# B11 + B12 in a seven-product SwiGLU matmul: the vector engine's addition replaced by a DMA transfer that adds on arrival

## The chip, the cores and the metric

The kernel runs on one core of one Trainium2 chip. The metric is the device time of one execution in microseconds. A core has a matrix engine (PE), a vector engine (DVE), a scalar engine (ACT), GpSimd (POOL) and SyncE (SP). Each works through its own list of instructions in order and waits at the head of that list for semaphores of the others. Transfers are issued from the lists of SP, ACT or POOL and are carried out by 16 DMA engines that all of them share.

## The reference, cut to what matters

One layer of a trunk with 512 latent tokens and 256 context tokens of width 2048. The change lies in the channel mixer, in the first product of `swiglu`, whose weight is 2048 x 11264 (5632 columns for `a`, 5632 for `b`):

```python
def swiglu(h, w_in, w_out):
    a, b = jnp.split(h @ w_in, 2, axis=-1)
    return (jax.nn.silu(a) * b) @ w_out

def trunk_layer(...):
    ...
    x = x + mod_x[2] * rms_norm(y_x, g_post_mix)
    f_x = swiglu(modulate(rms_norm(x, g_pre_ffn), mod_x[3], mod_x[4]), w_ffn_in, w_ffn_out)
    x = x + mod_x[5] * rms_norm(f_x, g_post_ffn)
```

## The kernel before

The layer runs stage by stage: modulation vectors, input projections, the gated linear attention, the output projection (`wo`, to about 930 us of the span), the first SwiGLU product (`f0` to `f10`, about 950 to 1850 us), the second one (`fo`, `fz`, to the end). Every float32 operand is split into a rounded high part and a remainder (`parts`, L992 to L997: ACT casts the high part, DVE subtracts for the low part), and each product is three matmuls: high by high, low by high, high by low.

The first SwiGLU product is cut into 11 groups of 512 columns of `a` and the 512 columns of `b` beside them (`ffn_group(gi)`, tiles named `f0...` to `f10...`). In a group the weight is a 2 x 2 matrix of blocks: B11 and B21 are the upper and lower 1024 rows of the `a` columns, B12 and B22 those of the `b` columns. The tokens are cut in two halves as well. The 2 x 2 product is made with seven block products in place of eight, from sums of blocks; the sums of the activations (`S1` to `S7`) are made once, those of the weights in every group. Each block comes in four pieces q = 0 to 3 of 256 rows, and a piece is one SBUF tile of 128 x 1024 float32, 512 KB, loaded by one transfer issued from SP (`wide`, L999, through `load`, L195).

The products of a group and the names of their pieces, in order:

- product 1, from B11: `X` is loaded and its parts are `a0` to `a3`. Groups 0 to 2 have products 1 (and mostly 2) done early, from another copy of the block; there `X` is only loaded, ahead of the sum.
- product 2, from B21: `b0` to `b3`.
- product 5, from B11 + B12: `c` is loaded and added into `X` (L1225); the parts of `X` are now `c0` to `c3`.
- product 6: `d` (B22) is added into `X` (L1232). Product 4: `e` (B21 again) is added into `X` (L1241).
- products 3 and 7: `z` (B22) and `y` (B12), with one sum `y + z` (L1255).

Four sets of buffers set the pace: `X` has 4 tiles, the loaded pieces `R` (for b, c, d, e, z, y) have 4, and the high and the low parts have 3 each. A load waits until its buffer's last reader is done, and so does a cast into a part's buffer, whose last reader is PE. A background generator (`gate_ffn`) reads more weight rows (`m50w` to `m53w`) between the groups; its accumulators are cleared by a memset on POOL.

The order in which each engine does its work is written when the program is built, by a scheduler that goes by the program's order, by the buffers that are free and by modelled durations.

Of the kernel before, what the change touches and what calls it, by code (L numbers as in the profile page):

```python
# [15 lines left out]
ALU = mybir.AluOpType  # L16
AX = mybir.AxisListType

P = 128
# [6 lines left out]
HID = 5632  # L26
# [65 lines left out]
def trunk_kernel(ctx, tc, cmat, cmask, x, c, ctxt, c_ctx, w_mod, b_mod, g_pre_mix, g_post_mix, g_pre_ffn,  # L92
                 g_post_ffn, w_in, ln_g, ln_b, w_s, b_s, wd2_f, bd_f, wd2_b, bd_b, out_g, w_out, w_ffn_in,
                 w_ffn_out, out):
    nc = tc.nc
    V, S, T, G = nc.vector, nc.scalar, nc.tensor, nc.gpsimd
# [64 lines left out]
    def rstd_exp(ss, n, name):  # L161

        s1 = cp.tile([P, n], F32, tag=f"s{n}", bufs=4, name=name + "s")
        v = cp.tile([P, n], F32, tag=f"rv{n}", bufs=2, name=name + "v")
        r = cp.tile([P, n], F32, tag=f"rr{n}", bufs=4 if n == 1 else 2, name=name + "r")
        t = cp.tile([P, n], F32, tag=f"rt{n}", bufs=2, name=name + "t")
        V.tensor_reduce(out=s1, in_=ss, axis=AX.X, op=ALU.add)
        S.activation(r, s1, AF.Ln, bias=eps, scale=1.0 / D)
        S.activation(r, r, AF.Exp, scale=-0.5)
        V.tensor_scalar(out=v, in0=s1, scalar1=1.0 / D, scalar2=EPS, op0=ALU.mult, op1=ALU.add)  # L170
        newton(v, r, t)
        return r
# [108 lines left out]
    def pump():  # L281
        bg.step()
        bgm.step()
# [406 lines left out]
    for o in (0, 512):  # L690
        n = min(512, len(LEVELS) * P - o)
# [290 lines left out]
    def fslot(name, dt=F32):  # L982
        return fp.tile([P, 512], dt, tag="f", bufs=NF, name=name)

    def chain_tile(name):
        return fp.tile([P, 1024], F32, tag="X", bufs=4, name=name)

    def raw2(name):
        return st2.tile([P, 1024], F32, tag="R", bufs=4, name=name)

    def parts(src, name):

        wh = st2.tile([P, 1024], F32R, tag="wh", bufs=3, name=name + "h")
        wl = st2.tile([P, 1024], F32R, tag="wl", bufs=3, name=name + "l")
        S.copy(wh, src)  # L995
        V.tensor_tensor(out=wl, in0=src, in1=wh.bitcast(F32), op=ALU.subtract)  # L996
        return wh, wl  # L997

    def wide(w, r, c0, t, name):  # L999

        load(t.rearrange("p (k c) -> p k c", k=2), w[r:r + 2 * P, c0:c0 + 512].rearrange("(k p) c -> p k c", p=P))
        return t
# [145 lines left out]
    def product(p, q, accs, wp, nq):  # L1148
        hi, lo = SP[p][q]
        for j in range(2):  # L1150
            for t in range(2):
                c = slice(j * 256 + t * P, j * 256 + (t + 1) * P)
                three(accs[t], (hi[:, c], lo[:, c]), cut(wp, j * 512, 512), q == 0 and j == 0, q == nq - 1 and j == 1)

    def two(name):
        return [bank(f"{name}{t}") for t in range(2)]
# [5 lines left out]
    def vtt(out, a, b, op):  # L1162
        for i in range(2):
            V.tensor_tensor(out=out[i], in0=a[i], in1=b[i], op=op)

    def blk(gi, i, j, q, t):

        return wide(w_ffn_in[0], i * (D // 2) + 2 * q * P, (gi * 512, HID + gi * 512)[j], t, f"f{gi}")

    def ffn_top(gi, new):  # L1170

        n = f"f{gi}"
        raw = [None] * NQ
        ps = two(n + "p1")
        for q in range(NQ):
            raw[q] = blk(gi, 0, 0, q, new(f"{n}X{q}"))
            product(1, q, ps, parts(raw[q], f"{n}a{q}"), NQ)
            pump()
        u = [fslot(f"{n}u{t}") for t in range(2)]
        for t in range(2):  # L1180
            S.copy(u[t], ps[t])
        turn_hidden()
        return u, raw

    def ffn_top2(gi, u):

        n = f"f{gi}"
        ps = two(n + "p2")
        for q in range(NQ):
            product(2, q, ps, parts(blk(gi, 1, 0, q, raw2(f"{n}b{q}")), f"{n}b{q}"), NQ)  # L1190
            pump()
        a1 = [fslot(f"{n}g{t}") for t in range(2)]
        vtt(a1, ps, u, ALU.add)
        for t in range(2):
            S.activation(a1[t], a1[t], AF.Silu)
        turn_hidden()
        return a1
# [15 lines left out]
    def ffn_group(gi):  # L1213
        n = f"f{gi}"
        if gi >= 3:
            u, X = ffn_top(gi, chain_tile)
        else:
            u = early_u[gi]
            X = [blk(gi, 0, 0, q, chain_tile(f"{n}X{q}")) for q in range(NQ)]
        a1 = ffn_top2(gi, u) if gi >= 2 else early_a[gi]  # L1220

        p5 = two(n + "p5")
        for q in range(NQ):
            r = blk(gi, 0, 1, q, raw2(f"{n}c{q}"))
            V.tensor_tensor(out=X[q], in0=X[q], in1=r, op=ALU.add)  # L1225
            product(5, q, p5, parts(X[q], f"{n}c{q}"), NQ)
            pump()
        turn_hidden()
        p6 = two(n + "p6")
        for q in range(NQ):  # L1230
            r = blk(gi, 1, 1, q, raw2(f"{n}d{q}"))
            V.tensor_tensor(out=X[q], in0=X[q], in1=r, op=ALU.add)  # L1232
            product(6, q, p6, parts(X[q], f"{n}d{q}"), NQ)
            pump()
        vtt(u, u, p6, ALU.subtract)
        u4 = [fslot(f"{n}w{t}") for t in range(2)]
        vtt(u4, p5, u, ALU.add)
        p4 = two(n + "p4")
        for q in range(NQ):
            r = blk(gi, 1, 0, q, raw2(f"{n}e{q}"))  # L1240
            V.tensor_tensor(out=X[q], in0=X[q], in1=r, op=ALU.add)  # L1241
            product(4, q, p4, parts(X[q], f"{n}e{q}"), NQ)
            pump()
        vtt(u, p4, u, ALU.add)
        if gi == HID // 512 - 1:
            for _ in range(8):
                gT.append(next(src))

        p7, p3 = two(n + "p7"), two(n + "p3")
        for q in range(NQ):  # L1250
            z = blk(gi, 1, 1, q, raw2(f"{n}z{q}"))
            y = blk(gi, 0, 1, q, raw2(f"{n}y{q}"))
            product(3, q, p3, parts(z, f"{n}z{q}"), NQ)
            pump()
            V.tensor_tensor(out=y, in0=y, in1=z, op=ALU.add)  # L1255
            product(7, q, p7, parts(y, f"{n}y{q}"), NQ)
        vtt(u, u, p7, ALU.subtract)
        for t in range(2):
            S.activation(u[t], u[t], AF.Silu)
        vtt(p7, p7, u4, ALU.subtract)  # L1260
        vtt(u4, p3, u4, ALU.subtract)
        vtt(a1, a1, u4, ALU.mult)
        vtt(u, u, p7, ALU.mult)
        behind.append((gi, a1 + u))
# [3 lines left out]
    def turn_hidden():  # L1268

        while behind:  # L1270
            gi, toks = behind.pop()
            n = f"f{gi}"
            for f in range(4):
                ps = bank(f"{n}T{f}", False)
                for t in range(NT):
                    T.transpose(ps[:, t * P:(t + 1) * P], toks[t][:, f * P:(f + 1) * P], ident)
                gt = slot(f"{n}t{f}")
                S.copy(gt, ps)
                nc.scalar.dma_start(g_dr[gi * 4 + f], gt)
# [8 lines left out]
    for gi in range(HID // 512):  # L1288
        if gi == 3:
            bgm.add(gate_ffn())  # L1290
        ffn_group(gi)
# [51 lines left out]
    for t in range(NT):  # L1343
# [5 lines left out]
        for cg in range(4):  # L1349
# [3 lines left out]
            f = facc[t][cg]  # L1353
# [4 lines left out]
        r = rstd_exp(fss, 1, f"er{t}")  # L1358
# [32 lines left out]
```

## Time and profile before

| | |
|---|---|
| median of 3 runs | 2351.94 us (2342.42 to 2353.6) |
| the profiled execution's own time | 2349.05 us |
| its span | 2347.2 us |
| PE busy | 2262.3 us (96%) |
| PE weight loads busy | 1836.9 us (78%) |
| DVE busy | 1593.5 us (68%) |
| ACT busy | 982.2 us (42%) |
| POOL busy | 15.5 us (1%), 24 instructions |
| moved by DMA | 477.30 MB, mean 203 GB/s |

The busy time of an engine is given for the whole span. Stages have different limits, so the rows below are taken stretch by stretch. PE's matmuls overlap, and a PE row's busy time counts their modelled ends; PE's real losses show as waits and in the granted clock.

### The profile page before, as it was taken

How to read it: one execution, taken by the hardware profiler on the slowest of the kernel's cores; microseconds unless marked ns; L12 is line 12 of the kernel's file. 1: busy time of each engine (PE TensorE's matmuls, PEld its weight loads, DVE VectorE, ACT ScalarE, POOL GpSimd, SP SyncE). 2: the span in 40 equal slices, each digit the busy share in tenths (PEclk: the TensorE clock that was granted, in tenths of full speed). 3: DMA queues.
4: the chain of work that ended last, by engine and by line, in shares of the span. 5: the costliest groups of instructions: out<-in, count | busy, mean ns of one | idle time of the engine just before them, and what ended most of it. 6: DMA issues, size and time to landing. Idle time of an engine off the chain costs nothing.

```text
span 2347.2 us, 27855 instructions
## 1 busy us (share of the span) xinstructions
PE 2262.3 (96%) x10386; PEld 1836.9 (78%) x10386; DVE 1593.5 (68%) x2072; ACT 982.2 (42%) x1509; POOL 15.5 (1%) x24
## 2 busy tenths in 40 slices
PE   7999998999999989989999999999999999999998
PEld 2778887788878867767788877788888788888886
DVE  3886587677795655798878877887888732242346
ACT  4444234465565315853444444344444432241232
POOL 0000000000000000000000000000000000000000
PEclk9999999999999999999999999999999999999999
DMA  9967788844452785756666756776686642253344
GB/s 324 329 217 236 239 294 275 266 159 126 155 182 86 251 286 182 226 186 225 218 210 220 244 192 209 248 232 203 199 261 198 234 144 98 93 182 104 109 139 156
DMA packets 252012, 477.30 MB, mean 203 GB/s; under 512 B 21162, under 2 KB 32642, under 8 KB 251876
## 3 DMA queue, kind: packets, MB, share of 16 engines
q1 hardware_dynamic: 241152, 457.78, 59.6%
q10 hardware_dynamic: 10724, 17.74, 2.1%
q8 instruction: 81, 1.33, 0.2%
q14 instruction: 55, 0.45, 0.1%
HBM read 451.33 MB, written 24.13 MB: 203 GB/s over the span
## 4 chain that ended last, share of the span: by engine, by line
PE 64%; DMA 15%; DVE 15%; issue 3%; ACT 2%; SPq 0%; DVEq 0%; ACTq 0%
PE fo L116 19%; PE wo L116 4%; PE f1p L116 3%; PE f9p L116 3%; PE f2p L116 3%; PE vv1a L116 2%; PE u1a L116 2%; PE fz L116 2%; PE cv L116 2%; PE g1a L116 2%; PE f7p L116 2%; PE q L116 2%; PE vv0a L116 2%; PE u L116 2%; PE g0a L116 2%
## 5 line engine op out<-in xcount | busy, mean ns | idle before, releaser
L1207 DVE TENSOR_TENSOR gl<-gr,gh 128x512 fp32r<-128x512 f32 x44 | 28.4, 686 | 24.7 <-ACT gh L1206 24.7
L1206 ACT CAST gh<-gr 128x512 fp32r<-128x512 f32 x44 | 25.1, 618 | 33.3 <-DMA gr<-g_dr 26.4
L832 ACT ACTIVATE lv<-lv 128x1024 f32<-128x1024 f32 x20 | 21.0, 1057 | 21.6 <-DVE lv L831 21.6
L229 DVE SCALAR_TENSOR_TENSOR m20acc<-m20w,cpair,m20acc 128x1024 f32<-128x1024 f32 x16 | 20.5, 1284 | 12.6 <-DMA m20w<-in_w_mod_dram 12.4
L996 DVE TENSOR_TENSOR fo_2l<-fo_r,fo_2h 128x1024 fp32r<-128x1024 f32 x8 | 9.8, 1225 | 27.0 <-ACT fo_2h L995 27.0
L116 PE MATMUL g1a<-hxh,g_0h 128*128 128x512 f32 x64 | 27.4, 429 | 0.3 <-ACT g_0h L277 0.3
L996 DVE TENSOR_TENSOR fo_8l<-fo_r,fo_8h 128x1024 fp32r<-128x1024 f32 x8 | 9.8, 1226 | 26.2 <-ACT fo_8h L995 26.2
L116 PE MATMUL vv0a<-vv_0h,hxh 128*128 128x512 f32 x64 | 27.6, 434 | 0.0
L996 DVE TENSOR_TENSOR fo_18l<-fo_r,fo_18h 128x1024 fp32r<-128x1024 f32 x8 | 9.8, 1226 | 26.1 <-ACT fo_18h L995 26.1
L996 DVE TENSOR_TENSOR fo_0l<-fo_r,fo_0h 128x1024 fp32r<-128x1024 f32 x8 | 9.8, 1223 | 25.5 <-ACT fo_0h L995 25.5
L1355 ACT ACTIVATE junk<-fc 128x512 bf16<-128x512 f32 x16 | 10.1, 631 | 40.4 <-DVE fc L1354 40.3
L116 PEld LDWEIGHTS s<-lv 128*128 128x128 f32 x192 | 25.0, 191 | 2.4 <-issue 0.5
L116 PE MATMUL g0a<-hxh,g_0h 128*128 128x512 f32 x64 | 26.8, 419 | 0.0
L996 DVE TENSOR_TENSOR fo_16l<-fo_r,fo_16h 128x1024 fp32r<-128x1024 f32 x8 | 9.8, 1225 | 24.7 <-ACT fo_16h L995 24.7
L116 PE MATMUL vv1a<-vv_0h,hxh 128*128 128x512 f32 x64 | 26.3, 426 | 0.0
L996 DVE TENSOR_TENSOR fo_10l<-fo_r,fo_10h 128x1024 fp32r<-128x1024 f32 x8 | 9.8, 1224 | 24.1 <-ACT fo_10h L995 24.1
L116 PE MATMUL vv0a<-vv_0l,hxh 128*128 128x512 f32 x64 | 26.1, 408 | 0.0
L116 PE MATMUL vv0a<-vv_0h,hxl 128*128 128x512 f32 x64 | 26.0, 407 | 0.0
L996 DVE TENSOR_TENSOR fo_14l<-fo_r,fo_14h 128x1024 fp32r<-128x1024 f32 x8 | 9.8, 1224 | 23.9 <-ACT fo_14h L995 23.9
L229 DVE SCALAR_TENSOR_TENSOR m21acc<-m21w,cpair,m21acc 128x1024 f32<-128x1024 f32 x16 | 20.5, 1282 | 7.9 <-DMA m21w<-in_w_mod_dram 7.3
L996 DVE TENSOR_TENSOR fo_12l<-fo_r,fo_12h 128x1024 fp32r<-128x1024 f32 x8 | 9.8, 1226 | 23.5 <-ACT fo_12h L995 23.5
L116 PE MATMUL g0a<-hxh,g_0l 128*128 128x512 f32 x64 | 25.7, 402 | 0.0
(3875 smaller groups left out, 7969.8 us busy)
## 6 DMA issues: line engine op xcount, KB each, us to landing
fo_r<-in_w_ffn_out_dram SPq DMA_DIRECT2D x80, 512.0 KB
gr<-g_dr SPq DMA_DIRECT2D x22, 512.0 KB
mx4w<-in_w_mod_dram SPq DMA_DIRECT2D x16, 512.0 KB
mx8w<-in_w_mod_dram SPq DMA_DIRECT2D x16, 512.0 KB
mx12w<-in_w_mod_dram SPq DMA_DIRECT2D x16, 512.0 KB
mc4w<-in_w_mod_dram SPq DMA_DIRECT2D x16, 512.0 KB
mc8w<-in_w_mod_dram SPq DMA_DIRECT2D x16, 512.0 KB
mc12w<-in_w_mod_dram SPq DMA_DIRECT2D x16, 512.0 KB
```

The lines of the kernel that those rows point to most:

```text
L116: return T.matmul(o, lhsT=l, rhs=r, start=start, stop=stop)
L229: ins = V.scalar_tensor_tensor(out=acc, in0=raw[:, j].rearrange("p i c -> p (i c)"), scalar=cvec[:, k0 + j:k0 + j + 1], in1=acc, op0=ALU.m ...
L832: S.activation(lv, lv, AF.Exp)
L996: V.tensor_tensor(out=wl, in0=src, in1=wh.bitcast(F32), op=ALU.subtract)
L1206: S.copy(hi, r[:, j * 512:(j + 1) * 512])
L1207: V.tensor_tensor(out=lo, in0=r[:, j * 512:(j + 1) * 512], in1=hi.bitcast(F32), op=ALU.subtract)
L1355: S.activation(junk, f, AF.Square, accum_out=fss[:, cg:cg + 1])
```

## The change

In each of the 11 groups the four loads of `c` from SP into an `R` buffer and the four additions on DVE go. In their place POOL issues four transfers that read the same 512 KB of B12 and add it to what stands in `X`. What followed, the parts `c0` to `c3` and product 5, is as it was.

```diff
         p5 = two(n + "p5")
         for q in range(NQ):
-            r = blk(gi, 0, 1, q, raw2(f"{n}c{q}"))
-            V.tensor_tensor(out=X[q], in0=X[q], in1=r, op=ALU.add)
+            nc.gpsimd.dma_start(X[q].rearrange("p (k c) -> p k c", k=2),
+                                w_ffn_in[0][2 * q * P:(2 * q + 2) * P, HID + gi * 512:HID + (gi + 1) * 512].rearrange(
+                                    "(k p) c -> p k c", p=P), accum_op=ALU.add)
             product(5, q, p5, parts(X[q], f"{n}c{q}"), NQ)
             pump()
```

Group 7 stands here for groups 3 to 10; its three queues change as follows. First DVE, from the low part of the second piece of B21 on, before the change (the number behind an underscore is a tile's serial number):

```order
L996 TENSOR_TENSOR f7b1l_12532<-f7b1_12529,f7b1h_12531 128x1024
L1225 TENSOR_TENSOR f7X0_12398<-f7X0_12398,f7c0_12594 128x1024
L1225 TENSOR_TENSOR f7X1_12416<-f7X1_12416,f7c1_12613 128x1024
L229 SCALAR_TENSOR_TENSOR m51acc_11370<-m51w15_12547,cpair_76,m51acc_11370 128x512
L996 TENSOR_TENSOR f7b2l_12553<-f7b2_12550,f7b2h_12552 128x1024
L996 TENSOR_TENSOR f7b3l_12571<-f7b3_12568,f7b3h_12570 128x1024
L1225 TENSOR_TENSOR f7X2_12434<-f7X2_12434,f7c2_12632 128x1024
L996 TENSOR_TENSOR f7c0l_12598<-f7X0_12398,f7c0h_12597 128x1024
L1225 TENSOR_TENSOR f7X3_12455<-f7X3_12455,f7c3_12651 128x1024
L996 TENSOR_TENSOR f7c1l_12617<-f7X1_12416,f7c1h_12616 128x1024
```

And DVE from the same place with the change:

```order
L996 TENSOR_TENSOR f7b1l_12476<-f7b1_12473,f7b1h_12475 128x1024
L229 SCALAR_TENSOR_TENSOR m51acc_11328<-m51w15_12491,cpair_76,m51acc_11328 128x512
L996 TENSOR_TENSOR f7b2l_12497<-f7b2_12494,f7b2h_12496 128x1024
L996 TENSOR_TENSOR f7b3l_12515<-f7b3_12512,f7b3h_12514 128x1024
L996 TENSOR_TENSOR f7c0l_12540<-f7X0_12342,f7c0h_12539 128x1024
L1233 TENSOR_TENSOR f7X0_12342<-f7X0_12342,f7d0_12614 128x1024
L996 TENSOR_TENSOR f7c1l_12557<-f7X1_12360,f7c1h_12556 128x1024
```

The four additions of `c` are gone, two of which stood ahead of `b2l`; the additions of `d` follow more closely. PE takes the products of groups 3 to 9 in the same order in both programs.

POOL with the change, at group 7, with what each instruction waits for (DMAHW: a load from SP or ACT, DMASW: a transfer from POOL); before, only the memset stood here:

```order
L1224 DMA f7X0_12342<-in_w_ffn_in_dram 128x2x512 [waits DMAHW2_49,DMASW0_49,DVE_49]
L1224 DMA f7X1_12360<-in_w_ffn_in_dram 128x2x512 [waits DMAHW3_49,DMASW1_49,DVE_49]
L1224 DMA f7X2_12378<-in_w_ffn_in_dram 128x2x512 [waits DMASW2_49,DMAHW6_49,DVE_49,Activation_49]
L1224 DMA f7X3_12399<-in_w_ffn_in_dram 128x2x512 [waits DMAHW7_49,DMASW3_49,DVE_49]
L221 MEMSET m52acc_12690 128x512 [waits DMAHW5_49,DMAHW1_49,DMAHW0_49]
```

Each adding transfer waits for the low part of product 1 on DVE, the last reader of `X` as it was. The memset of `m52acc` now stands behind the fourth of them.

SP from the last piece of `b` on, before the change:

```order
L195 DMA f7b3_12568<-in_w_ffn_in_dram 128x2x512
L195 DMA f7c0_12594<-in_w_ffn_in_dram 128x2x512
L195 DMA f7c1_12613<-in_w_ffn_in_dram 128x2x512
L203 DMA m51w15_12547<-in_w_mod_dram 128x512
L195 DMA f7c2_12632<-in_w_ffn_in_dram 128x2x512
L195 DMA f7c3_12651<-in_w_ffn_in_dram 128x2x512
L195 DMA f7d0_12678<-in_w_ffn_in_dram 128x2x512
L195 DMA f7d1_12697<-in_w_ffn_in_dram 128x2x512
```

And with it:

```order
L195 DMA f7b3_12512<-in_w_ffn_in_dram 128x2x512
L195 DMA f7d0_12614<-in_w_ffn_in_dram 128x2x512
L195 DMA f7d1_12633<-in_w_ffn_in_dram 128x2x512
L203 DMA m51w15_12491<-in_w_mod_dram 128x512
L195 DMA f7d2_12652<-in_w_ffn_in_dram 128x2x512
L195 DMA f7d3_12671<-in_w_ffn_in_dram 128x2x512
L195 DMA f7e0_12704<-in_w_ffn_in_dram 128x2x512
```

The loads of `d` take the places, and the `R` buffers, that the loads of `c` had.

## Rows read from the trace of the kernel before

**Rows 1.** The page: busy time of each engine, share of the span, instructions.

```profile
PE 2262.3 (96%) x10386; PEld 1836.9 (78%) x10386; DVE 1593.5 (68%) x2072; ACT 982.2 (42%) x1509; POOL 15.5 (1%) x24
```

**Rows 2.** Busy time by stretch: group 7, and the sum over five such groups.

```profile
core 0: us, PE busy (x) PEld busy (x) DVE busy (x) ACT busy (x) POOL busy (x), PEclk, DMA share, GB/s
...
1530.21:1610.49 80.28, 79.78 (x355) 64.92 (x355) 66.41 (x70) 34.75 (x38) 0.00 (x0) 1.00 0.68 219
...
sum 404.41, PE 397.69 PEld 323.61 DVE 333.88 ACT 174.06 POOL 1.05; mean PE 79.54 PEld 64.72 DVE 66.78 ACT 34.81 POOL 0.21
```

**Rows 3.** The chain that ended last, in order of time: start, us, work.

```profile
1010.07 2.86 DVE f0X L1225 x3
...
1144.03 5.95 DMA f2c<-in_w_ffn_in_dram
...
1542.43 3.74 DMA f7c<-in_w_ffn_in_dram
```

**Rows 4.** The tile `f7X`: duration ns min/median/max, first and last start us.

```profile
L195 SPq DMA_DIRECT2D f7X<-in_w_ffn_in_dram x4: 367/372/379, 1495.0 to 1503.1; - x4
L1225 DVE TENSOR_TENSOR f7X<-f7X,f7c x4: 1219/1226/1226, 1542.8 to 1552.7; 128x1024 f32<-128x1024 f32 x4
...
L996 DVE TENSOR_TENSOR f7a0l<-f7X,f7a0h x1: 1224/1224/1224, 1525.9 to 1525.9; 128x1024 fp32r<-128x1024 f32 x1
...
L996 DVE TENSOR_TENSOR f7a1l<-f7X,f7a1h x1: 1225/1225/1225, 1528.6 to 1528.6; 128x1024 fp32r<-128x1024 f32 x1
...
L996 DVE TENSOR_TENSOR f7a2l<-f7X,f7a2h x1: 1215/1215/1215, 1535.7 to 1535.7; 128x1024 fp32r<-128x1024 f32 x1
L996 DVE TENSOR_TENSOR f7a3l<-f7X,f7a3h x1: 1215/1215/1215, 1536.9 to 1536.9; 128x1024 fp32r<-128x1024 f32 x1
L995 ACT CAST f7c0h<-f7X x1: 1047/1047/1047, 1548.7 to 1548.7; 128x1024 fp32r<-128x1024 f32 x1
...
L995 ACT CAST f7c1h<-f7X x1: 1057/1057/1057, 1552.1 to 1552.1; 128x1024 fp32r<-128x1024 f32 x1
...
L995 ACT CAST f7c2h<-f7X x1: 1054/1054/1054, 1554.9 to 1554.9; 128x1024 fp32r<-128x1024 f32 x1
...
L995 ACT CAST f7c3h<-f7X x1: 1053/1053/1053, 1557.6 to 1557.6; 128x1024 fp32r<-128x1024 f32 x1
```

**Rows 5.** Instructions in order of time, group 7: start, us, engine, work, [idle before <-releaser].

```profile
1539.26 3.55 SPq L195 DMA_DIRECT2D f7c<-in_w_ffn_in_dram  x2
...
1542.79 1.23 DVE L1225 TENSOR_TENSOR f7X<-f7X,f7c 128x1024 f32<-128x1024 f32 x1 [0.38 <-DMA f7c<-in_w_ffn_in_dram]
...
1546.19 1.23 DVE L1225 TENSOR_TENSOR f7X<-f7X,f7c 128x1024 f32<-128x1024 f32 x1 [2.18 <-DMA f7c<-in_w_ffn_in_dram]
...
1549.27 0.19 PEld L116 LDWEIGHTS f7p<-f7b2l,S2h 128*128 128x128 f32 x1 [0.79 <-DVE f7b2l L996]
```

**Rows 6.** Busy time by stretch, group 7, between product 1 and product 5.

```profile
1527.00:1539.00 12.00, 12.00 (x59) 9.73 (x58) 10.51 (x15) 6.23 (x8) 0.00 (x0) 1.00 0.25 90
1539.00:1558.00 19.00, 18.63 (x85) 15.16 (x84) 14.45 (x15) 9.92 (x13) 0.00 (x0) 1.00 0.86 289
```

**Rows 7.** Busy time by stretch, group 0, where the last token sums are made.

```profile
1004.00:1034.00 30.00, 23.43 (x98) 17.64 (x97) 30.00 (x38) 17.01 (x27) 0.00 (x0) 0.89 0.50 166
```

**Rows 8.** PE's waits, 930 to 1870 us: us in total, times, longest.

```profile
PE f0p L116 <- DVE f0d0l L996: 2.3, 1, 2.3
PE f0p L116 <- ACT f0d0h L995: 2.0, 1, 2.0
PE f2p L116 <- DVE f2c0l L996: 1.8, 1, 1.8
...
PE f5p L116 <- DVE f5c3l L996: 1.2, 1, 1.2
...
PE f6p L116 <- DVE f6b2l L996: 0.5, 1, 0.5
...
PE f9p L116 <- DVE f9b2l L996: 0.3, 1, 0.3
```

## Prediction, made before the changed kernel ran

> **What bounds the kernel now.** I read the page first. PE is busy 96% of the span, DVE 68%, POOL 1% [rows 1], so time can only be won where PE waits. The change touches only the first SwiGLU product; there I looked at the groups one by one. Group 7 takes 80.28 us, PE is busy for 79.78 of them at the full granted clock (1.00, the 2.4 GHz level), DVE for 66.41, the DMA engines for 0.68 of the time; in five such groups PE is idle 404.41 - 397.69 = 6.72 us, 1.34 a group [rows 2]. In these groups PE itself is the bound, and work taken off DVE is worth a small part of itself. The chain of waits says where it is more: it runs over the additions of `c` in group 0, over a load of `c` in group 2, and over one in group 7 [rows 3]. Group 0 is the exception: between 1004 and 1034 us DVE is busy 30.00 of 30.00 us, PE only 23.43, and the clock's mean is 0.89, because PE, left idle there, was granted the lower level (1.2 GHz) for part of the stretch [rows 7]. DVE is the bound there.
>
> **What the change removes.** (1) 44 additions (4 in each of 11 groups) of 1.22 us [rows 4] are 54 us of DVE work. Beside PE nearly all of it is covered. On the path lie:
>
> Group 0. Three of its four additions lie in the DVE-bound stretch (the chain gives them 2.86 us [rows 3]), and one just before it. PE idles 30 - 23.43 = 6.57 us there; two waits, for `d0`, make up 2.3 + 2.0 of it [rows 8]. The low clock costs another 30 x 0.11 = 3.3 us. The most that can come back is 9.9 us, the least nothing (PE's list there is rearranged too: three pieces of `d` now stand ahead of `c3`). I take half, **5.0 us**: four additions are 4.9 us off a chain in which DVE never rests.
>
> Group 2. PE waits 1.8 us for `c0`'s low part [rows 8], behind the load of 5.95 us in the chain [rows 3]. With the change `X` is ready long before, since nothing reads it between its load and the sum. **1.8 us**.
>
> Groups 3 to 10. In DVE's list two additions stand ahead of `b2l`, and the second sits 2.18 us on its load; PE then waits 0.79 us for its weights [rows 5]. Seven such waits for `b2l` are listed, from 0.5 down to 0.3 us, in total 2.8, and one of 1.2 us for `c3l` of group 5 [rows 8]. With the additions gone nothing on DVE stands between `b1l` and `b2l` but one short piece of background work. **4.0 us**; the most is all of PE's idle time, 8 x 1.34 = 10.7 us, the least nothing, if other waits take their places.
>
> (2) 44 loads go from SP's list. Their `R` buffers pass to `d`. But SP's next load still waits for `b0`'s low part to free a buffer, as now, so `d0` starts when `c0` starts now (1539.26 [rows 5]). `d` is not needed earlier: 0 us.
>
> **What it adds.** 44 transfers from POOL. The same bytes are read from the weight; the target is read as well. No row of this kernel shows a transfer that adds, so I bound its time A from issue to landing. From below: a plain load of the same 512 KB, issued at 1539.26 and used at 1542.79, 3.5 us [rows 5]. From above: that load, an addition of 1.2 us, and a second pass as long as the load for reading and writing the target, 8.3 us. The DMA engines move 219 GB/s at a share of 0.68 [rows 2], so at full share 322, and 0.524 MB occupies them for 1.6 us. An addition reads a second stream of the same size, so I take A = 3.5 + 1.6 = 5.2 us, nearer the plain load because only the stream grows, not what surrounds it. The Trainium skill says the same of the mechanism ("Collectives: The Full Stack", the bandwidth ceiling): an add in the DMA path costs no cycles of its own but needs two source reads and runs at half rate. By "DMA: Bandwidth & Descriptors", anatomy of one DMA, a plain POOL transfer of this size takes some 2.0 + 1.2 = 3.2 us, an estimate from its formula; neither moves the sum.
>
> Is A hidden? In group 7 the four pieces of `X` are free of readers at 1527.1, 1529.8, 1536.9 and 1538.1 us (start plus duration of `a0l` to `a3l`), and the casts that need the sums start at 1548.7, 1552.1, 1554.9 and 1557.6; what holds those casts now is PE, which frees the parts' buffers [rows 4]. Each transfer has 18 to 22 us. Even strictly one after another they have 1557.6 - 1527.1 = 30.5 us, so the cover holds **up to A = 7.6 us**. The engines have room: from 1527 to 1539 their share is 0.25, from 1539 to 1558 it is 0.86 [rows 6], which leaves 9.0 + 2.7 us, and the four loads of `c` leave another 6.5; four transfers of 3.3 us need 13. So 0 us. If the cover goes, `c0h` to `c3h` are late on ACT, and behind them on its in-order list the SiLU of the group and the casts of `d`; on DVE `c0l` holds up the additions of `d`. PE then waits for product 5, one for one.
>
> On POOL's list the memset of an accumulator now stands behind the fourth transfer in four groups. Its user on DVE stands behind `c3l`, whose cast starts 19 us after that transfer can be issued; 0 us. The next load of `X` on SP now also waits for a transfer of the group before, whose sum product 5 has long used by then: 0 us.
>
> **The sum.** -5.0 - 1.8 - 4.0 = -10.8 us on the profiled execution's 2349.05, which makes 2338.3. The median of the runs shown stands 2.9 us above that execution, so the forecast is **2341 us**, -0.46%. About 0.5%, 11.8 us, is what a measurement of this kernel can tell from no change; the forecast lies just inside.
>
> **Rivals.** *DVE relief is worth more.* Group 0 gives back all 9.9 us, with its clock, and groups 3 to 10 all of PE's idle time: 9.9 + 1.8 + 10.7 = 22.4 us, 2330. For it: DVE's share of 30.00 in 30.00, and that `c`'s loads wait at the busiest time of the DMA engines (0.86). Against it: PE's idle time has other owners too. Between the two ends lies 2335.
>
> *The adding transfer is slow, and product 5 waits for it* (the rival on the other side). It decides in groups 3 to 10, at the cast of `c3`, from A = 7.6 us on if the four run one after another. Each of eight groups then loses 4A - 30.5 us, and only group 0's and 2's 6.8 us are kept: A = 8.3 gives 8 x 2.7 - 6.8 = +15, 2367; A = 9 gives +37, 2389; A = 12 gives +133, 2485. For it: the trace shows no such transfer, and the margin over my A is under 1.5. Against it: the pieces become free in pairs into a stretch at share 0.25, and doubled engine time fits.
>
> *POOL cannot prepare its transfers while DVE works.* DVE is idle for 1.49 of the 12 us and 4.55 of the 19 us before product 5 [rows 6], 1.5 us for each of four. SP needs 0.37 us for an issue [rows 4]; if POOL needs over 1.5 us and only gets DVE's pauses, the last sum is late by the rest: at 2.5 us, 4 us in each of eight groups, 32 - 6.8 = +25, 2377. Against it: what runs on DVE there are additions and subtractions of 1024 float32 in 1.22 us, about one element per cycle. The Trainium skill's "SBUF — State Buffer", summary of rules, speaks against issuing from POOL under DVE work (descriptor generation starves while DVE is in a two-port mode), but its section on who interferes with whom says `tensor_tensor` has no such mode; by that the rule does not bite here.
>
> That the transfer copies and does not add would not show in the time: A would be 3.5, and the forecast the same.
>
> **How the numbers follow.** Hidden, with a gain of up to 11.8 us: 0.41. Hidden, with more: 0.32. Slow transfer: 0.20. POOL held up: 0.07. The likeliest case gives 2341; its own range is 2340 to 2352. The range to hold 8 in 10 runs from 2328 (nearly all of the first rival) to 2390 (A = 9); above it I leave some 0.12 to 0.15, below it 0.04. Faster 0.32, same 0.41, slower 0.27.
>
> **What would show it.** Right: the transfers of POOL land within 7.6 us of their issue, and in group 7 the casts `c0h` to `c3h` still follow PE, not a DMA; the waits of PE for `b2l` and for `c0l` of group 2 are gone; between 1004 and 1034 us PE idles some 3 to 5 us less and the granted clock is above 0.89; a group takes 79.5 to 80 us. Wrong: waits of ACT or DVE on `X` for a DMA ahead of product 5, groups of over 81 us, a lower granted clock in groups 3 to 10, or POOL's transfers issued long after `a3l` ended.

## The result, and the profile after

The changed kernel takes **2379.7 us** (median of 4 runs, 2377.24 to 2385.45) against 2352.77 for the kernel before beside it: ratio **1.0128 [1.0093, 1.0162]**, slower by some 27 us. The forecast was 2341 us. The time lies in its range, on the other side of no change.

Two places of the page: the busy times, which answer to [rows 1], and the DMA queues (packets, MB, share of 16 engines' span):

```profile
PE 2272.5 (96%) x10386; PEld 1847.5 (78%) x10386; DVE 1548.5 (65%) x2028; ACT 981.2 (41%) x1509; POOL 68.8 (3%) x68
...
q1 hardware_dynamic: 229184, 434.71, 56.0%
q0 software_dynamic: 11968, 23.07, 5.8%
```

DVE has lost 44 instructions and 45 us, and PE is slower all the same: its 10386 matmuls are busy for 10.2 us more than before. PE's waits from 930 to 1900 us (us in total, times, longest) answer to [rows 8]:

```profile
PE f10p L116 <- DVE f10b2l L996: 5.2, 1, 5.2
PE f9p L116 <- DVE f9b2l L996: 5.0, 1, 5.0
PE f3p L116 <- DVE f3b2l L996: 4.8, 1, 4.8
PE f8p L116 <- DVE f8b2l L996: 4.6, 1, 4.6
PE f7p L116 <- DVE f7b2l L996: 4.5, 1, 4.5
PE f6p L116 <- DVE f6b2l L996: 4.4, 1, 4.4
PE f4p L116 <- DVE f4b2l L996: 4.4, 1, 4.4
PE f1p L116 <- DVE f1y1l L996: 4.2, 1, 4.2
PE f0p L116 <- DVE f0y2l L996: 2.2, 1, 2.2
```

The waits for `d0` in group 0 and for `c0l` in group 2 are gone. But `b2l`, 2.8 us over seven waits before, now costs 32.9 us over seven: in groups 3 to 10 with one exception, group 5. Only there does no background load stand on SP between the loads of `d`. What DVE's waits (same columns) name is the background work:

```profile
DVE m50acc L229 <- DMA m50w<-in_w_mod_dram: 21.8, 4, 9.4
DVE m52acc L229 <- DMA m52w<-in_w_mod_dram: 20.1, 5, 9.6
DVE m51acc L229 <- DMA m51w<-in_w_mod_dram: 19.5, 3, 9.0
...
DVE m53acc L229 <- DMA m53w<-in_w_mod_dram: 10.7, 3, 9.7
```

Group 7 shows how. POOL's, SP's and DVE's lists there, in order of time (start, us, instruction, [idle before <-releaser]):

```profile
1546.28 2.45 POOL L1224 DMA_DIRECT2D f7X<-in_w_ffn_in_dram  x2 [6.16 <-ACT f6t L1279]
...
1548.04 3.53 SPq L195 DMA_DIRECT2D f7d<-in_w_ffn_in_dram  x2
...
1549.96 1.23 DVE L996 TENSOR_TENSOR f7b1l<-f7b,f7b1h 128x1024 fp32r<-128x1024 f32 x1 [1.94 <-ACT f7b1h L995]
...
1551.63 0.51 SPq L203 DMA_DIRECT2D m51w<-in_w_mod_dram  x1
...
1560.22 0.75 DVE L229 SCALAR_TENSOR_TENSOR m51acc<-m51w,cpair,m51acc 128x512 f32<-128x512 f32 x1 [9.04 <-DMA m51w<-in_w_mod_dram]
1560.89 1.22 DVE L996 TENSOR_TENSOR f7b2l<-f7b,f7b2h 128x1024 fp32r<-128x1024 f32 x1
...
1562.14 1.50 SPq L195 DMA_DIRECT2D f7d<-in_w_ffn_in_dram  x2
```

The same load in the kernel before:

```profile
1541.18 1.23 DVE L996 TENSOR_TENSOR f7b1l<-f7b,f7b1h 128x1024 fp32r<-128x1024 f32 x1 [1.95 <-ACT f7b1h L995]
...
1542.85 0.46 SPq L203 DMA_DIRECT2D m51w<-in_w_mod_dram  x1
...
1547.34 0.75 DVE L229 SCALAR_TENSOR_TENSOR m51acc<-m51w,cpair,m51acc 128x512 f32<-128x512 f32 x1
1548.00 1.22 DVE L996 TENSOR_TENSOR f7b2l<-f7b,f7b2h 128x1024 fp32r<-128x1024 f32 x1
```

Before, the 256 KB of `m51w` had landed at most 1547.34 - 1542.85 = 4.5 us after their issue, since DVE did not wait for them; now it takes 1560.22 - 1551.63 = 8.6 us (8.5 to 9.3 in groups 3, 4 and 6 to 10). Just ahead of them stand two loads of `d` and two adding transfers. DVE's list is worked in order: the accumulation waits 9.04 us at its head, `b2l` behind it, and PE behind `b2l`. In both kernels the load is issued 0.44 us after `b1l` ends. From the end of `b1l` to the start of `b2l` it is 5.6 us before and 9.7 us now: 4.1 us more, as much as the load lands later. PE's wait for this `b2l` goes from 0.3 to 0.5 us [rows 8] to 4.5.

Stretches of this kernel (us; busy time and count of PE, PEld, DVE, ACT, POOL; granted clock, DMA share, GB/s):

```profile
1004.00:1034.00 30.00, 28.10 (x122) 22.06 (x121) 29.55 (x35) 18.43 (x29) 0.27 (x1) 0.94 0.49 143
1550.00:1555.00 5.00, 5.00 (x26) 4.18 (x25) 1.18 (x1) 3.28 (x6) 0.00 (x0) 1.00 1.08 245
1555.00:1560.00 5.00, 2.68 (x12) 1.88 (x10) 0.00 (x0) 1.92 (x2) 0.00 (x0) 1.00 1.06 349
1560.00:1565.00 5.00, 2.83 (x7) 2.23 (x8) 4.74 (x5) 0.00 (x0) 0.00 (x0) 0.75 0.35 103
```

From 1550 to 1560 us the DMA engines are full, DVE does nothing in the second half, and after PE's pause the mean granted clock is 0.75, so part of that stretch ran at the lower level (1.2 GHz). The first row answers to [rows 7]: group 0 did what was forecast, PE idles 1.9 us there in place of 6.57.

The ledger: group 3 begins 2.8 us earlier than before (1203.9 against 1206.7), product 3 of group 10 begins 29.7 us later (1860.2 against 1830.5). So groups 3 to 10 lost 32.5 us. These are the two stretches (columns as above), before and now:

```profile
1206.70:1830.50 623.80, 613.02 (x2728) 499.15 (x2727) 519.96 (x549) 272.64 (x303) 1.58 (x3) 1.00 0.68 219
1203.90:1860.20 656.30, 623.15 (x2728) 509.02 (x2728) 486.97 (x516) 272.15 (x303) 39.16 (x34) 0.98 0.72 208
```

PE idles 33.2 us in place of 10.8, which is 22.4 us more: the `b2l` waits grew by 30.1, and other waits shrank. The other 10.1 us are PE's busy time for the same 2728 matmuls, at a mean granted clock of 0.98 in place of 1.00. So about a third of the loss is the lower clock, as in the last row of group 7 above.

### The profile page after: what moved, and what is told of

It is laid out like the page before. It is cut to its first block, busy times and chain, and to the rows that moved or that the text cites. A ratio compares the mean times of both kernels' runs of the same rounds, so it can differ in the third digit from the quotient of the medians.

```text
span 2375.1 us, 27898 instructions
## 1 busy us (share of the span) xinstructions
PE 2272.5 (96%) x10386; PEld 1847.5 (78%) x10386; DVE 1548.5 (65%) x2028; ACT 981.2 (41%) x1509; POOL 68.8 (3%) x68
## 3 DMA queue, kind: packets, MB, share of 16 engines
q1 hardware_dynamic: 229184, 434.71, 56.0%
q0 software_dynamic: 11968, 23.07, 5.8%
## 4 chain that ended last, share of the span: by engine, by line
PE 79%; DMA 10%; DVE 6%; ACT 2%; issue 2%; SPq 0%; ACTq 0%; DVEq 0%
PE fo L116 18%; PE wo L116 3%; PE f5p L116 3%; PE f3p L116 3%; PE f7p L116 3%; PE f9p L116 3%; PE f8p L116 3%; PE f6p L116 3%; PE f2p L116 3%; PE f1p L116 3%; PE f4p L116 3%; PE f10p L116 2%; PE vv1a L116 2%; PE v0a L116 2%; PE u1a L116 2%; PE fz L116 2%
## 5 line engine op out<-in xcount | busy, mean ns | idle before, releaser
L229 DVE SCALAR_TENSOR_TENSOR mc4acc<-mc4w,cpair,mc4acc 128x1024 f32<-128x1024 f32 x16 | 20.5, 1284 | 10.0 <-DMA mc4w<-in_w_mod_dram 9.7
L1356 ACT ACTIVATE junk<-fc 128x512 bf16<-128x512 f32 x16 | 10.1, 631 | 40.4 <-DVE fc L1355 40.3
L116 PE MATMUL v1a<-v_0h,hxh 128*128 128x512 f32 x64 | 26.4, 413 | 0.0
L229 DVE SCALAR_TENSOR_TENSOR m50acc<-m50w,cpair,m50acc 128x512 f32<-128x512 f32 x16 | 12.0, 748 | 21.9 <-DMA m50w<-in_w_mod_dram 21.8
L116 PE MATMUL v1a<-v_0l,hxh 128*128 128x512 f32 x64 | 25.8, 403 | 0.0
```

The source lines that it names most:

```text
L116: return T.matmul(o, lhsT=l, rhs=r, start=start, stop=stop)
L229: ins = V.scalar_tensor_tensor(out=acc, in0=raw[:, j].rearrange("p i c -> p (i c)"), scalar=cvec[:, k0 + j:k0 + j + 1], in1=acc, op0=ALU.m ...
L1356: S.activation(junk, f, AF.Square, accum_out=fss[:, cg:cg + 1])
```

## The experiments

**Theory 1**: an adding transfer occupies the shared DMA engines for a second stream; a background load that stands behind two `d` loads and beside these transfers lands late, its accumulation blocks `b2l` on DVE, PE stops. **Theory 2**: transfers from POOL cost this as such, added or not. **Theory 3**: product 5 waits for its sums.

The table gives for each run the time, the ratio to the kernel before on the same chip, and from its profile the time from the first matmul on `c0` of group 0 to that on `a0` of group 3, and from there to `a0` of group 10 (seven groups). The last column is the steadiest: it leaves out the stages ahead, whose length differs by up to 12 us from one profile to the next. Kernels with the same transfers differ by some 3 us in it (591.4 and 594.5; 574.7, 571.3 and 572.1).

| kernel | us | ratio [95%] | groups 0 to 2 | seven groups |
|---|---|---|---|---|
| before (2346.54 in the one run beside e9 to e11) | 2349 to 2353 | | 195.9 | 563.7 |
| the change | 2379.7 | 1.0128 [1.0093, 1.0162] | 194.6 | 591.4 |
| e1 plain copies | 2346.32 | 0.9984 [0.9968, 1.0000] | 185.5 | 574.7 |
| e2 change, background later | 2331.08 | 0.9919 [0.9903, 0.9936] | 190.8 | 548.2 |
| e3 before, background later | 2327.0 | 0.9908 [0.9889, 0.9928] | 198.8 | 549.0 |
| e4 half the additions | 2335.04 | 0.9945 [0.9930, 0.9960] | 193.5 | 559.3 |
| e5 change, accumulations later | 2334.06 | 0.9923 [0.9898, 0.9947] | 192.5 | 551.3 |
| e6 before, accumulations later | 2336.95 | 0.9943 [0.9924, 0.9962] | 196.0 | 551.0 |
| e7 half, background later | 2332.71 | 0.9918 [0.9896, 0.9939] | 193.7 | 548.6 |
| e8 groups 0 to 2 only | 2345.64 | 0.9983 [0.9970, 0.9997] | 191.3 | 561.6 |
| e9 change with a probe | 2380.79, one run | | 194.9 | 594.5 |
| e10 plain copies again | 2350.31, one run | | 187.7 | 571.3 |
| e11 plain copies with a probe | 2347.78, one run | | 190.1 | 572.1 |

**e1: the same transfers without the addition.** The order of all engines' lists stays as in the change.

```diff
-                                    "(k p) c -> p k c", p=P), accum_op=ALU.add)
+                                    "(k p) c -> p k c", p=P))
```

> The change with the addition left out of the POOL transfer: it overwrites X with B12, so product 5 and what follows get B12 in place of B11 + B12; the order of instructions on every engine is that of the change. Theory 1 (the second stream that an adding transfer reads occupies the DMA engines, 3.13 us a transfer against 1.60 for a load in the changed kernel's trace; a background load of w_mod queued behind it is late, and on DVE it stands ahead of b2l, for which PE waits): the background load lands about 2 x 1.5 = 3 us earlier, PE's wait for b2l falls from 4.4 to 5.2 us to about 1.5, a group from 85 us to about 82, the time to about 2358 (2350 to 2365). Theory 2 (any transfer issued from POOL holds up the others, adding or not): as the change, 2375 to 2382. Theory 3 (product 5 waits for the sums themselves): casts of c0 to c3 stop waiting, but the waits for b2l stay as they are, 2370 to 2380.

2346.32 us, 4 us below theory 1's interval and far from the change's time. The row of its page on POOL's queue:

```profile
q0 software_dynamic: 6336, 23.07, 3.1%
```

and SP and DVE in its group 7, in order of time:

```profile
1522.30 1.22 DVE L996 TENSOR_TENSOR f7b1l<-f7b,f7b1h 128x1024 fp32r<-128x1024 f32 x1 [1.96 <-ACT f7b1h L995]
...
1523.97 0.46 SPq L203 DMA_DIRECT2D m51w<-in_w_mod_dram  x1
...
1530.32 0.75 DVE L229 SCALAR_TENSOR_TENSOR m51acc<-m51w,cpair,m51acc 128x512 f32<-128x512 f32 x1 [6.80 <-DMA m51w<-in_w_mod_dram]
1530.99 1.22 DVE L996 TENSOR_TENSOR f7b2l<-f7b,f7b2h 128x1024 fp32r<-128x1024 f32 x1
```

The same 23.07 MB take the engines 3.1% in place of 5.8% of the span, in 6336 packets in place of 11968. The page lists the same bytes for both, so that the doubled time is a second read is not shown by these rows. The background load is usable 6.35 us after its issue (5.6 to 7.4 in groups 3, 4 and 6 to 10 of e1, e10 and e11): between the 4.5 us of before and the 8.6 of the change. From the end of `b1l` to `b2l` it is 7.5 us, 1.9 more than before, and PE waits 2.2 us for `f7b2l`.

The last column says the same: +11.0 us on the kernel before with copies (e10: +7.6, e11: +8.4), +27.7 with additions; a group takes 82.1 us, as expected. So the addition makes the larger part. The smaller part belongs to the transfers without it. Whether it comes because POOL issues them (theory 2), or because two more transfers of 512 KB now run beside the background load, from whatever queue, no run tells apart. Groups 0 to 2 are 6 to 10 us shorter with copies than in the kernel before, which about cancels this, and the total comes out level.

**e2 and e3: the background work of the gates moved behind the groups**, into the second product, in the change and in the kernel before.

```diff
-        if gi == 3:
-            bgm.add(gate_ffn())
         ffn_group(gi)
     bgm.drain()
+    bgm.add(gate_ffn())
+    bgm.rate = 0.6
...
     bg.drain()
+    bgm.drain()
```

> The change, with the background generator gate_ffn (the w_mod loads m50w to m53w and their sums on DVE) moved behind the groups, into the second SwiGLU product. Theory 1: the waits for b2l are gone in all groups, each takes 79 to 79.5 us as group 5 does now, in which no background load stands ahead of b2l; 7 groups x 5.5 = 38 us come back, less 0 to 5 for the background work in its new place: 2338 to 2348. Theory 2 or 3: groups stay at 83 us or more, 2370 or more.

> The kernel before, with the same generator moved to the same place. Theory 1: it gains little, since its background loads are in time: PE's short waits, and the 82.8 us of group 5 against 80.3 of the others, come to 3 to 7 us, 2345 to 2350; it stands 3 to 12 us above the change with the same move. Theory 2 or 3: it stands 20 us or more below the change with the same move.

e2 comes out at 2331.08, 7 us below theory 1's interval: without background loads in the groups the adding transfers cost nothing there (548.2 us against 549.0), and theory 3 falls with it. A group takes 548.2 / 7 = 78.3 us in e2 and 78.4 in e3. The expectation for e3 was the larger miss: the kernel before gains 22 us from the same move. The two intervals overlap; the adding transfer wins nothing that shows once the background is out of its way.

**e4: two of four.** Pieces 0 and 1 added by transfer, pieces 2 and 3 loaded and added on DVE as before.

```diff
+            if q < 2:
                 nc.gpsimd.dma_start(X[q]..., accum_op=ALU.add)
+            else:
+                r = blk(gi, 0, 1, q, raw2(f"{n}c{q}"))
+                V.tensor_tensor(out=X[q], in0=X[q], in1=r, op=ALU.add)
```

> The adding transfer for q = 0 and 1 alone; q = 2 and 3 are loaded from SP and added on DVE as before. Theory 1: the first two fall into the stretch in which the DMA engines are least busy and are done before the background load is issued; it lands as before, PE's wait for b2l is under 1 us, groups take 79.5 to 80.5 us, 2338 to 2350. Theory 2: about half of the loss stays, 2360 to 2370.

2335.04, 3 us below theory 1's interval, and faster than the kernel before (of the 13.8 us between the two profiled executions, 6.8 lie in the two columns, the rest outside them). Pieces 0 and 1 become free first; their transfers run in the stretch where the DMA engines stood at 0.25 before [rows 6], and the waits for `b2l` are 0.4 to 0.7 us. The loads and additions of pieces 2 and 3 stand where those of 0 and 1 stood before, ahead of the background load's accumulation. So e4 shows that two early adding transfers do no harm; how much of the change's loss is the addition's it can't show.

**e5 and e6: only DVE's order.** Adding transfers and background loads keep their places on POOL and SP, but for one load that comes later where one accumulator ends and the next begins. Each background accumulation is issued one step later and kept there, so that the one ahead of `b2l` belongs to a load that landed long ago; the late load's accumulation stands behind `c0l`. e6 is the same in the kernel before.

```diff
-            for j in range(per):
-                ins = V.scalar_tensor_tensor(out=acc, in0=raw[:, j]...)
+            waiting.append((k0, raw))
+            if k0 or not ahead:
+                q0, raw = waiting.pop(0)
+                for j in range(per):
+                    ins = V.scalar_tensor_tensor(out=acc, in0=raw[:, j]...)
+                    if ahead or pin and q0 + j == 0:
+                        tc.keep_in_program_order(ins)
             yield None
```

> All four adding transfers stay, and all background loads stay in the groups and in their places on SP; only the background accumulations (m50acc to m53acc) stand one step later on DVE, so that the one before b2l belongs to a load issued far earlier, and the late load's own accumulation stands behind c0l. Theory 1 (the late load stops PE only through its accumulation ahead of b2l on DVE's list): the seven b2l waits of 4.4 to 5.2 us fall under 1 us each, each of those groups takes about the 79.5 us that group 5 took in the changed kernel, 7 x (85.3 - 79.5) = 41 us: 2339 us (2334 to 2346). Rival (it is the amount of background transfers beside the adding ones, in whatever order DVE reads them): the wait turns up at c0l, c1l or a d load instead, 2360 to 2380 us.

> The kernel before with the same later background accumulations, as the control. Theory 1: its seven b2l waits were 2.8 us together and little else hung on the accumulations, so 2344 to 2352 us. If the kernel before also loses its 2 us per group (80.3 against the 78.3 of the runs with the background moved out) to accumulations that wait on DVE, 2330 to 2337 us.

e5 takes 2334.06, just inside theory 1's interval, and PE waits for no `b2l` in groups 3 to 10. Group 7 of e5, SP and DVE in order of time (its line numbers stand 5 higher):

```profile
1531.85 0.75 DVE L234 SCALAR_TENSOR_TENSOR m51acc<-m51w,cpair,m51acc 128x512 f32<-128x512 f32 x1
...
1532.38 0.55 SPq L203 DMA_DIRECT2D m51w<-in_w_mod_dram  x1
...
1535.53 1.23 DVE L1001 TENSOR_TENSOR f7b2l<-f7b,f7b2h 128x1024 fp32r<-128x1024 f32 x1 [2.93 <-ACT f7b2h L1000]
...
1541.46 0.75 DVE L234 SCALAR_TENSOR_TENSOR m51acc<-m51w,cpair,m51acc 128x512 f32<-128x512 f32 x1 [0.91 <-DMA m51w<-in_w_mod_dram]
```

This is the run that settles it. The late load is as late as in the change, 1541.46 - 1532.38 = 9.1 us, and costs DVE 0.91 us and PE nothing, because `b2l` no longer stands behind it. The load is late beside full DMA engines; the place of one accumulation turns that into PE's lost time. e6, 2336.95, lies in the second interval: the kernel before gains 12.7 us in the seven groups by the same order, far more than its 2.8 us of `b2l` waits. The seven groups before and in e6 (columns as in the stretches above):

```profile
1206.70:1770.40 563.70, 555.72 (x2471) 452.79 (x2471) 466.70 (x488) 243.16 (x266) 1.58 (x3) 1.00 0.68 221
1202.80:1753.80 551.00, 550.79 (x2470) 453.35 (x2470) 465.48 (x485) 244.13 (x266) 1.58 (x3) 1.00 0.69 224
```

PE idles 0.2 us in place of 8.0 and is busy 4.9 us less for as many matmuls (one record fewer). Which of the accumulations the rest hung on was not tried apart. Against e6 as its control the change costs 551.3 - 551.0 = 0.3 us in the seven groups, where in the old order it costs 27.7.

**e7 and e8.** e7 joins e4 and e2's move. e8 has all four adding transfers in groups 0 to 2 alone (`if gi < 3:` where e4 has `if q < 2:`).

> Adding transfers for q = 0 and 1 alone, q = 2 and 3 loaded and added by DVE as before, and the last gates' background work moved behind the groups. Theory 1: nothing but PE is left to bound a group, 78.3 us each as with four or with no adding transfers: 2325 to 2333 us. If the early groups' relief of DVE adds to that without the late y loads of four transfers, 2320 to 2325 us.

> All four adding transfers in groups 0 to 2, where no background work of the gates runs; groups 3 to 10 as in the kernel before. Group 3 began at 1203.9 us in the changed kernel and at 1206.7 in the kernel before. Theory 1 (all the loss is in groups 3 to 10): 2343 to 2349 us beside 2350 for the kernel before. As the prediction's terms had it for groups 0 and 2 (-6.8): 2342 to 2345. If adding transfers cost by themselves wherever they stand: over 2352.

e7, 2332.71, is not told apart from e2 and e3: PE bounds all three in the seven groups (548.2 to 549.0 us). e8 shows what relieving DVE in the early groups is worth: 2345.64 against 2349.11, 3.5 us less, with an interval of 0.7 to 7.0, inside theory 1's expectation and just short of the prediction's terms. Its PE still waits 4.6 us for `f1y1l`.

**e9 to e11: how long an adding transfer takes.** A copy of one column of `X3` on POOL stands behind the fourth transfer and can start when that has landed; in e11 the transfers are plain copies. e10 is e1 again.

```diff
+        nc.gpsimd.tensor_copy(junk[:, gi:gi + 1], X[3][:, 1023:1024])
         turn_hidden()
         p6 = two(n + "p6")
```

> The changed kernel with one more POOL instruction per group: a copy of one column of the fourth tile X3, which can start only when the fourth adding transfer has landed, so that its start less the start of that transfer's issue is the time A that the prediction had to estimate (5.2 us, 3.5 to 8.3). Theory 1 (a transfer alone moves its block twice, 3.1 us of engine time, and shares the engines with the loads issued around it): 5 to 9 us, and the kernel's time as the change's, 2372 to 2386 us. If the adding transfers were what product 5 waits for, A would be over 15 us.

> The changed kernel unaltered but for plain copies in place of additions (as e1_copy, leaving out the addition of B11 + B12), run again beside e9 on the same chip. Theory 1: 2340 to 2352 us.

> Plain POOL copies in place of adding transfers (leaving out the addition of B11 + B12), with the same one-column copy of X3 behind them. Theory 1 (without the second stream the transfer takes what the kernel before's loads of the same block took): 3.5 to 6 us from issue to landing, at least 1.5 us less than with the addition; 2338 to 2352 us.

POOL in group 7 of e9, with additions:

```profile
1550.38 1.21 POOL L1224 DMA_DIRECT2D f7X<-in_w_ffn_in_dram  x1 [0.27 <-issue]
1560.46 0.18 POOL L1229 CAST junk<-f7X 128x1 bf16<-128x1 f32 x1 [8.87 <-DMA f7X<-in_w_ffn_in_dram]
```

and of e11, with copies:

```profile
1531.45 0.72 POOL L1224 DMA_DIRECT2D f7X<-in_w_ffn_in_dram  x1 [0.41 <-issue]
1538.66 0.18 POOL L1229 CAST junk<-f7X 128x1 bf16<-128x1 f32 x1 [6.48 <-DMA f7X<-in_w_ffn_in_dram]
```

From issue to landing the fourth adding transfer takes 10.1 us and the fourth copy 7.2. Both are longer than expected (5 to 9, 3.5 to 6), as they stand in the crowded stretch; the difference, 2.9 us, is above the 1.5 us asked for. e9's time, 2380.79, is the change's, and e11's one run took 2347.78. The pages also list the median landing of a group's four transfers; here group 7 of the change and of e1:

```profile
f7X<-in_w_ffn_in_dram POOLq DMA_DIRECT2D x4, 512.0 KB, 8.3
...
f7X<-in_w_ffn_in_dram POOLq DMA_DIRECT2D x4, 512.0 KB, 5.2
```

In groups 3 to 10 it is 6.2 to 8.3 us in the change and 4.8 to 5.5 in e1: the fourth of group 7 lands later than the middle of its four.

## Why the prediction was wrong

**The step that failed** is "The engines have room ... So 0 us", together with "nothing on DVE stands between `b1l` and `b2l` but one short piece of background work". The room was counted over 12 and 19 us, but the 9.0 us of it in the first stretch lay almost wholly ahead of the times at which the last two pieces of `X` become free (1536.9 and 1538.1 us); and only the transfers of the group itself were counted, with product 5 as the sole customer. The piece of work is short by its 0.75 us on DVE alone. Its operand comes by a DMA, and that DMA stands on SP behind the two loads of `d` and beside two adding transfers. In place of 0 us, its landing went from at most 4.5 to 8.6 us after the issue; in place of -4.0 us, groups 3 to 10 lost 32.5 us. e5 against e6 shows that this one place in DVE's list carries the loss; e1, e10 and e11 show that most of it takes the addition: without it 7.6 to 11.0 of the 27.7 us are left in the seven groups.

**The order would have told half of it.** The two DVE lists before the prediction show the accumulation of `m51w15` ahead of `b2l`, and the SP lists show its load between `d1` and `d2`. Before, the second addition ahead of it waited 2.18 us for its own load [rows 5], and by the time the accumulation's turn came its operand was there. With the additions gone its turn comes at 1551.19, 0.44 us before its load is even issued. Had the load then landed after 4.5 us, the most that the rows of before allow, `b2l` would have started 0.44 + 4.5 + 0.67 = 5.6 us after `b1l` ended (an estimate; 0.67 us lie between the starts of the accumulation and of `b2l`). That is what it was before, so the -4.0 us had no firm ground: the accumulation could hold `b2l` as long as the two additions had. The load's later landing then made the loss.

**Group 0, -5.0 us.** Right in its mechanism: between 1004 and 1034 us PE idles 1.9 us in place of 6.57, at a clock of 0.94 in place of 0.89, and from product 5 to product 3 group 0 takes 35.1 us in place of 43.7. Too much in size: part goes back at once to `y` loads (waits for `f0y2l`, 2.2 us, and `f1y1l`, 4.2 us). Over groups 0 to 2 the change keeps 1.3 us in its profile, and e8 measures 3.5 us against the 6.8 of groups 0 and 2 together. **Group 2, -1.8 us**: the wait for `c0l` is gone as forecast.

**A, 5.2 us, hidden up to 7.6.** The engine time was right: 5.8% of 2375.1 us over 44 transfers is 3.13 us each, where the prediction took 3.3; a plain load takes 56.0% of 2375.1 us x 0.524 / 434.71 MB = 1.60 us. The ratio of 1.95 agrees with the half rate that the Trainium skill gives ("Collectives: The Full Stack", the bandwidth ceiling). The time to landing was mis-sized: the median of a group's four is 6.2 to 8.3 us in groups 3 to 10, and the fourth of group 7 takes 10.1, outside the bounds of 3.5 to 8.3. Those were built from one load in a stretch with a DMA share of 0.86 [rows 6]; from 1550 to 1560 us of the change it is 1.06 to 1.08. Yet product 5 did not wait: no cast of `c` waits for a transfer, neither in the change, where nearly all of them wait for PE, nor in e5, where PE is not held up. The 7.6 us held only for transfers strictly one after another, and these overlap.

**The rivals.** The slow adding transfer came true in its first half alone: A is past its point of 7.6 us for the fourth transfer (by the median of the four in one group of eight), and product 5 does not wait. That the time lies in the range is owed to this rival's bound of 2390, by a mechanism that did not come: luck. Two of the signs of being wrong came, groups of over 81 us (591.4 / 7 = 84.5) and a lower clock in groups 3 to 10 (0.98). POOL was not held up by DVE: the transfer of `X1` is issued 0.3 us after `a1l` ends (1538.92 against 1537.39 + 1.23). The rivals on the slower side had the sign, but what happened was not among them: a wait of background work, off the transfers' own path.

## What to carry to other kernels

When work moves into the DMA system, list not only who waits for the moved transfer but which other loads share its stretch, and whose instruction stands behind their consumers on an in-order engine; a cheap background instruction ahead of a critical one is as long as its load is late. Put such an instruction a step behind its load (some 46 us off the change in e5, 12 us off the kernel before in e6), and only then ask what the transfer saves: here nothing that shows, since 2327 us is reached without it (e3).

## What the runs showed of the hardware that was not expected

- An adding transfer of 512 KB occupies the DMA engines for 3.13 us and a plain POOL transfer for 3.1% x 2340 / 44 = 1.65 us, as a load from SP (1.60).
- A 256 KB load from SP behind two 512 KB loads lands at most 4.4 to 4.6 us after its issue in the kernel before, 5.6 to 7.4 us beside plain POOL transfers (e1, e10, e11), and 8.5 to 9.3 us beside adding ones (groups 3, 4 and 6 to 10).
- POOL is busy for 1.20 us to issue an adding transfer and 0.72 us for a plain one of the same shape; SP needs 0.37 us for the load [rows 4].
- DVE's additions and subtractions took 1.22 us with POOL issuing beside them, as before.
- In the 5 us before the clock fell PE was busy 2.68 us; the next 5 us ran at a mean of 0.75 of the full clock.
